# Masking decays by a minimum on VectorE, and moving copies and mask products to ScalarE, in a gated DeltaNet stage

## The chip, the cores and the metric

The program runs on one core of a Trainium2 chip. The engines of the core are named here as in the profile: PE is TensorE, DVE is VectorE, ACT is ScalarE, POOL is GpSimd, SP is SyncE, which issues the DMA transfers. The metric is the device time of one execution in microseconds (us), lower being better.

## The reference, cut to what matters

Two different transformer blocks run one after the other on a 1024 x 1024 activation. The first mixes tokens with a bidirectional gated DeltaNet (4 head pairs of 64 channels, chunks of 64 tokens) beside a spatial gating unit, then has a feed-forward part; the second is an S5 state-space block with a gated feed-forward. All products are in float32.

```
for l in range(DEPTH):
    h = rms_norm(x, norm_mix[l])
    proj = jnp.einsum("bsd,dc->bsc", h, w_in[l])
    q, k, v, z, b_f, b_b, a_f, a_b, su, sv = jnp.split(proj, SPLIT_POINTS, axis=-1)
    qkv = jax.nn.silu(short_conv(jnp.concatenate([q, k, v], axis=-1), conv_w[l]))
    o_a = bidir_gated_deltanet(qkv, z, b_f, b_b, a_f, a_b, a_log_fwd[l], dt_bias_fwd[l],
                               a_log_bwd[l], dt_bias_bwd[l], gdn_norm[l])
    o_b = spatial_gating(su, sv, sgu_v_norm[l], sgu_w[l], sgu_b[l], sgu_out_norm[l])
    mix = jnp.concatenate([o_a, o_b], axis=-1)
    x = x + jnp.einsum("bsc,cd->bsd", mix, w_out[l])
```

The change touches only the DeltaNet. Within a chunk of 64 tokens a decay matrix exp(g_i - g_j) weights the products of keys with keys and of queries with keys. It holds only for j on one side of i (lower triangle for the forward direction, upper for the backward one); elsewhere it must be zero.

## The kernel before, in words

Every float32 product is made of three products of split operands (high and low part); ACT writes the high part (line 318) and DVE the low part (line 319), for weights (`wr` to `wh`, `wl`) and activations.

The first stage, up to about 750 us, weaves two kinds of work on PE. One is dense work: the projections `mm` of line 611, whose weights come in pieces of 256 KB. The other is the DeltaNet of four head pairs, `pair_gdn`, of which two are open at a time (named L and R; pairs 0 and 2 use the buffers of L, pairs 1 and 3 those of R). A planner (`drive`) writes PE's instructions in a fixed order that follows estimated latencies; each engine runs its own instructions in order. The order on DVE, ACT and SP is set by the framework's scheduler when the program is built, so that an edit can move neighbouring instructions there.

For each pair the projections of q, k and v are taken out of PSUM on DVE (`raw`, line 753), convolved over tokens (lines 759 on ACT, 763 and 766 on DVE, result `cy` or a slot of `fbgkq`) and normalised; line 824 (ACT) and lines 826 and 830 (DVE) make the rows of log decays, which go to DRAM and come back spread over 64 partitions. Then `pair_gdn` runs these steps:

- decay: for four matrices (two kinds in `N` and `Am`, two directions; the tiles are named `ca`, `fbgkq`, `ca`, `de` in the profile) DVE adds a column term (line 899), POOL overwrites the forbidden triangle with -1e30 by two selects, one for each half of the partitions (line 903), and ACT takes the exponential (line 905).
- token_major: PE transposes keys (and later values) into PSUM (line 881, `tp`), eight pieces of 64 x 256 are copied to SBUF, half of them by ACT (line 887) and half by DVE (line 889).
- gram: PE multiplies keys and queries (`gram`, line 773), DVE multiplies by the decays (line 925).
- inverse: DVE inverts 32 x 32 triangles by 31 dependent steps (lines 955 and 957, tiles `stp` and `h`), transposes the result (lines 962, 963, 965) and masks it by two products with a constant of halves (line 968).
- lvl, wu, chain, out: small products on PE, with copies out of PSUM on ACT (lines 985 to 1044), a recurrence over chunks (lines 1072, 1075) and the output norm (lines 1107 to 1120; line 1111 is ACT's spread of the norm's factor, which PE then transposes as `orb`).

After that stage come the output projection, the feed-forward parts and the second block, which the change does not touch.

Of the kernel before, what the change touches and what calls it, by code (L numbers as in the profile page):

```python
# [7 lines left out]
F32 = mybir.dt.float32  # L8
F32R = mybir.dt.float32r
I32 = mybir.dt.int32  # L10
AF = mybir.ActivationFunctionType
ALU = mybir.AluOpType
# [4 lines left out]
P = 128  # L17
# [5 lines left out]
NC = 16  # L23
NEG = -1.0e30
# [102 lines left out]
class Ln:  # L127
# [77 lines left out]
    def bc(self):  # L205
        K = self.K
        self.rb = K.bcast(self.dgr)
        m = K.bcast(self.dgm)
        self.mb = K.tmp("cb")[:, :m.shape[-1]]
        K.A.activation(self.mb, m, AF.Copy)  # L210
# [41 lines left out]
class Kern:  # L252
# [396 lines left out]
    def gdn_consts(self):  # L649
        gc, I, V, G, A = self.gc, self.I, self.V, self.G, self.A  # L650
        self.rows = gc.tile([P, S], F32, tag="rows", name="rows", bufs=1)
        self.bk = gc.tile([P, 32], F32, name="bk")
        self.dma(self.bk, I["c_bk"])
        self.bq = gc.tile([P, 32], F32, name="bq")
        self.dma(self.bq, I["c_bq"])
        self.half2 = gc.tile([P, 2 + 48], F32, name="half2")[:, :2]
        self.dma(self.half2, I["c_half"])
        self.selc = gc.tile([P, 12], F32, name="selc")
        self.dma(self.selc, I["c_selc"])
        self.cwh = gc.tile([P, 60], F32, name="cwh")  # L660
        o, c = VOFF["conv"]
        V.tensor_scalar(self.cwh, self.vecs[:, o:o + c], 0.5, None, op0=ALU.mult)
        self.mcol = gc.tile([32, 1], F32, name="mcol")
        A.activation(self.mcol, self.vec("g_alog")[:32], AF.Exp)
        V.tensor_scalar(self.mcol, self.mcol, -1.0, None, op0=ALU.mult)
        self.heads = gc.tile([P, 2], F32, name="heads")
        G.memset(self.heads, 0.0)
        for h in range(2):
            G.memset(self.heads[64 * h:64 * h + 64, h:h + 1], 1.0)
        self.gh = gc.tile([P, 1], F32, name="gh")  # L670
        V.tensor_scalar(self.gh, self.vec("gdn_gain"), 0.5, None, op0=ALU.mult)

# [183 lines left out]
    def pair_gdn(self, p, st, R):  # L856
        V, A, G, T = self.V, self.A, self.G, self.T
        (kq, vtd), rd, col = st
        c3 = lambda t: t.rearrange("p (c k) -> p c k", k=64)
# [15 lines left out]
        def token_major(dst, src):  # L875

            d4 = dst.rearrange("p (b e k) -> p b e k", e=2, k=64)
            for h in range(2):
                ps = self.gps(R, [P, 4, 2, 64], "tp")
                for b in range(4):  # L880
                    T.transpose(ps[:, b].rearrange("p h k -> p (h k)"), src[:, (4 * h + b) * P:(4 * h + b + 1) * P], self.ident)
                yield 0.55, 0.0
                for e in range(2):
                    for hh in range(2):
                        o, i = d4[64 * hh:64 * hh + 64, 4 * h:4 * h + 4, e, :], ps[64 * e:64 * e + 64, :, hh, :]
                        if e == hh:
                            A.activation(o, i, AF.Copy)
                        else:
                            V.tensor_copy(o, i)

        N, Am = [a, b], [c_, d_]
        for v in range(2):
# [3 lines left out]
        for v in range(2):  # L896
            for d in range(2):
                rb = (N, Am)[v][d]
                self.late(V.tensor_tensor(c3(rb), c3(rb), bc(d), op=ALU.add))
                for hh in range(2):  # L900
                    sl = slice(64 * hh, 64 * hh + 64)
                    sg = 1 if d == 0 else -1
                    G.affine_select(c3(rb)[sl], c3(rb)[sl], pattern=[[0, NC], [sg, 64]], compare_op=ALU.is_ge,
                                    fill=NEG, base=0, channel_multiplier=-sg)
                A.activation(rb, rb, AF.Exp)
        yield 0.0, 5.0
        while p >= 2 and p - 2 not in self.done:
            yield 0.0, 3.0
        kp = e_
        yield from token_major(kp, K)  # L910
        yield 0.0, self.LAT_TM

# [48 lines left out]
        yc = K.rearrange("p (d c k) -> p d c k", d=2, k=32)  # L961
# [3 lines left out]
        V.transpose(f, K)  # L965
        Y = [g, hs]
        for d in range(2):
            V.tensor_tensor(Y[d].rearrange("p (c e k) -> p c e k", e=2, k=32),
                              yc[:, d].unsqueeze(2).to_broadcast([P, NC, 2, 32]),
                              self.half2.unsqueeze(1).unsqueeze(3).to_broadcast([P, NC, 2, 32]), op=ALU.mult)  # L970
        yield 0.0, 4.0

        self.mark(f"lvl{p}")
# [50 lines left out]
        W, U = [f, K], Y  # L1024
        KW = [a, kp]
        yield from token_major(vp, vt)
        yield 0.0, self.LAT_TM
        for d in range(2):
# [36 lines left out]
        for st in range(1, NC + 1):  # L1065
            if st < NC - 1:
                cp = [self.gps(R, [P, 64], "cp", d) for d in range(2)]
                for d in range(2):
                    c = (st, NC - 1 - st)[d]
# [7 lines left out]
            if st >= 9:  # L1077

                k = st - 9
                if k % 4 == 0:  # L1080
                    while self.held:
                        yield 0.0, 0.5
                    o = self.gps(R, [P, 8, 64], "ob", 2)
# [29 lines left out]
        for h in range(2):  # L1113
            rb = self.gps(R, [P, 4, P], "orb")
# [3 lines left out]
            sl = self.HS[h]  # L1118
# [1206 lines left out]
```

## Time and profile before

| | |
|---|---|
| median of 3 runs | 2756.83 us (2752.54 to 2758.98) |
| the profiled execution's own time | 2753.74 us |
| its span in the trace | 2751.8 us |
| busy shares of the span | PE 95%, DVE 67%, ACT 38%, POOL 10% |
| mean granted clock of PE, share of full speed | 0.969 |

The busy shares are means over the span. The page also cuts the span into 40 slices of 69 us; the first ten hold most of the stage that the change touches, and PE's digit there (its busy share in tenths) is between 6 and 9, where it is 9 in almost all later slices.

### The profile page before, as it was taken

The page shows a single profiled execution, that of the slowest core. Times are in us where ns is not written, and L with a number is a line of the kernel's source. Part 1 is how long each engine was busy: PE and PEld are TensorE (multiplying, and loading weights), DVE is VectorE, ACT ScalarE, POOL GpSimd, SP SyncE. Part 2 cuts the span into 40 slices and gives each one's busy share as a digit, 9 for nine tenths or more (in the row PEclk, how much of TensorE's full clock was granted, in tenths as well). Part 3 has the DMA queues.
Part 4 walks back from the last instruction along what each step waited for, and adds up shares of the span by engine and source line. Part 5 has one row for each costly group of instructions (what it writes and reads, how often), then busy time and mean ns, then how long its engine had stood idle before and what let it go on. Part 6 is the DMA issues. An engine that isn't in the chain of part 4 may idle for free.

```text
span 2751.8 us, 39513 instructions
## 1 busy us (share of the span) xinstructions
PE 2602.0 (95%) x14952; PEld 2088.2 (76%) x14952; DVE 1854.9 (67%) x3367; ACT 1044.6 (38%) x1721; POOL 279.5 (10%) x502
## 2 busy tenths in 40 slices
PE   7868988898899999999999999989999999999997
PEld 5656766676688888888788888868876888888885
DVE  7899768865696566655548778666597555564456
ACT  5433443432454445221236433452253333351222
POOL 0220011000000000299700001100000000000010
PEclk9989999999999999999999999999999999999998
DMA  3332143131234336454413624644322222242211
GB/s 104 101 93 66 56 119 108 46 126 40 86 105 139 117 105 209 125 169 151 140 53 115 197 95 150 200 163 136 113 67 73 88 74 91 92 166 80 92 47 61
DMA packets 298621, 299.71 MB, mean 109 GB/s; under 512 B 34912, under 2 KB 243936, under 8 KB 298176
## 3 DMA queue, kind: packets, MB, share of 16 engines
q1 hardware_dynamic: 298432, 297.20, 34.3%
q8 instruction: 117, 1.92, 0.3%
q14 instruction: 72, 0.59, 0.1%
HBM read 222.29 MB, written 74.58 MB: 108 GB/s over the span
## 4 chain that ended last, share of the span: by engine, by line
PE 75%; DVE 14%; DMA 3%; ACT 3%; issue 3%; POOL 1%; SPq 1%; ACTq 0%; DVEq 0%; POOLq 0%
PE mm L1325 34%; PE mm L1298 26%; PE mm L611 6%; PE wu L773 2%; DVE wl L319 1%; DVE stp L955 1%; DVE h L957 1%; DVE cy L763 1%; PE ob L773 1%; PE cp L773 1%; DVE res L216 1%; PE mm L1430 0%; DVE res L215 0%; PE mm L193 0%; DVE t L319 0%
## 5 line engine op out<-in xcount | busy, mean ns | idle before, releaser
L1325 PE MATMUL mm<-t,wh 128*128 128x512 f32 x1728 | 541.4, 394 | 11.9 <-DVE acc L1372 4.5
L318 ACT ACTIVATE wh<-wr 128x512 fp32r<-128x512 f32 (+1 forms) x386 | 236.1, 614 | 660.9 <-PE mm L1298 280.8
L319 DVE TENSOR_TENSOR wl<-wr,wh 128x512 fp32r<-128x512 f32 (+1 forms) x385 | 267.4, 695 | 214.1 <-ACT wh L318 212.9
L1325 PEld LDWEIGHTS mm<-t,wh 128*128 128x128 f32 x1728 | 325.6, 189 | 88.6 <-DVE acc L1372 6.5
L1325 PE MATMUL mm<-b,wh 128*128 128x512 f32 x1232 | 382.4, 392 | 3.3 <-ACT acc L1366 3.2
L1298 PE MATMUL mm<-fh,wh 128*128 128x512 f32 x880 | 345.2, 392 | 3.7 <-DVE res L1506 3.7
L1298 PE MATMUL mm<-fl,wh 128*128 128x512 f32 x880 | 342.5, 389 | 0.0
L1298 PE MATMUL mm<-fh,wl 128*128 128x512 f32 x880 | 342.5, 389 | 0.0
L1325 PE MATMUL mm<-t,wl 128*128 128x512 f32 x864 | 338.2, 391 | 0.0
L1325 PEld LDWEIGHTS mm<-b,wh 128*128 128x128 f32 x1232 | 231.6, 188 | 53.7 <-ACT acc L1366 4.6
L1325 PE MATMUL mm<-b,wl 128*128 128x512 f32 x616 | 240.2, 390 | 0.0
L318 ACT ACTIVATE wh<-ws 128x512 fp32r<-128x512 f32 x216 | 135.4, 630 | 256.6 <-PE mm L1325 233.4
L1298 PEld LDWEIGHTS mm<-fh,wh 128*128 128x128 f32 x880 | 165.2, 188 | 40.8 <-issue 4.0
L319 DVE TENSOR_TENSOR wl<-ws,wh 128x512 fp32r<-128x512 f32 x216 | 148.5, 690 | 70.2 <-ACT wh L318 69.9
L1298 PEld LDWEIGHTS mm<-fh,wl 128*128 128x128 f32 x880 | 165.2, 188 | 34.7
L1298 PEld LDWEIGHTS mm<-fl,wh 128*128 128x128 f32 x880 | 165.2, 188 | 34.1 <-issue 0.5
L1325 PEld LDWEIGHTS mm<-t,wl 128*128 128x128 f32 x864 | 163.4, 189 | 33.9
L611 PE MATMUL mm<-xh,wh 128*128 128x512 f32 (+1 forms) x400 | 172.0, 430 | 12.8 <-ACT wh L318 7.2
L611 PE MATMUL mm<-xl,wh 128*128 128x512 f32 (+1 forms) x400 | 168.0, 420 | 2.1 <-DVE xl L399 2.0
L611 PE MATMUL mm<-xh,wl 128*128 128x512 f32 (+1 forms) x400 | 168.8, 422 | 0.0
L1506 DVE TENSOR_TENSOR res<-mm,res 128x512 f32<-128x512 f32 x128 | 85.8, 683 | 74.1 <-PE mm L1298 74.1
L1325 PEld LDWEIGHTS mm<-b,wl 128*128 128x128 f32 x616 | 115.9, 188 | 24.5
(491 smaller groups left out, 4273.1 us busy)
## 6 DMA issues: line engine op xcount, KB each, us to landing
wr<-in_w_ff SPq DMA_DIRECT2D x76, 256.0 KB
wr<-in_w_ff SPq DMA_DIRECT2D x32, 512.0 KB
fl<-ffd SPq DMA_DIRECT2D x32, 512.0 KB
wr<-in_w_in SPq DMA_DIRECT2D x32, 512.0 KB
wr<-in_w_in SPq DMA_DIRECT2D x60, 256.0 KB
wr<-in_w_gate SPq DMA_DIRECT2D x22, 512.0 KB
wr<-in_w_up SPq DMA_DIRECT2D x22, 512.0 KB
fl<-hd SPq DMA_DIRECT2D x22, 512.0 KB
```

Source lines behind the costliest of these rows:

```text
L216: K.V.tensor_tensor(r, r, self.mb, op=ALU.subtract)
L318: self.A.activation(hi, src, AF.Copy)
L319: return (lo_eng or self.V).tensor_tensor(lo, src, hi.bitcast(F32), op=ALU.subtract)
L611: self.T.matmul(ps, a[:, t, :], b[:, sl], start=(first and j == 0), stop=(last and j == 2))
L763: V.scalar_tensor_tensor(y[:, a:b], raw[:, a + o:b + o], cw[:, k:k + 1], y[:, a:b], op0=ALU.mult, op1=ALU.add)
L773: self.T.matmul(out(s), lhsT(s), rhs(s), start=start, stop=stop)
L955: V.tensor_tensor(tm, X3[:, :, 0:j, j:j + 1].to_broadcast([P, 2, j, n]), T3[:, :, j:j + 1, m:16].to_broadcast([P, 2, j, n]), op=ALU.mult)
L957: V.tensor_tensor(T3[:, :, 0:j, m:16], T3[:, :, 0:j, m:16], tm, op=ALU.subtract)
L1298: self.T.matmul(ps, a, b[:, sl], start=(start and k + j == 0), stop=(stop and k == n - 1 and j == 2))
L1325: self.T.matmul(ps, a[:, k, :], b, start=(start and k + j == 0), stop=(k == 3 and j == 2), skip_group_check=True)
L1506: V.tensor_tensor(res[d][:, sl], self.mm(w, ffs[g], sl), res[d][:, sl], op=ALU.add)
```

## The change

Four edits, all in the DeltaNet. A constant `below` (128 x 2 x 64) is made once at the start: +1e30 where a decay is allowed, -1e30 where it isn't, one plane for each direction. The decays are masked by one minimum with that constant on DVE in place of two selects on POOL. All eight copies of each token_major group go to ACT, where four were on DVE. The two mask products behind the inverse become four scaled copies on ACT, one for each direction and half.

```
+        self.below = gc.tile([P, 2, 64], F32, name="below")
+        G.memset(self.below, -NEG)
+        for d in range(2):
+            for hh in range(2):
+                sl = slice(64 * hh, 64 * hh + 64)
+                sg = 1 - 2 * d
+                G.affine_select(self.below[sl, d, :], self.below[sl, d, :], pattern=[[sg, 64]], compare_op=ALU.is_ge,
+                                fill=NEG, base=0, channel_multiplier=-sg)
...
-                        if e == hh:
-                            A.activation(o, i, AF.Copy)
-                        else:
-                            V.tensor_copy(o, i)
+                        A.activation(o, i, AF.Copy)
...
-                for hh in range(2):
-                    sl = slice(64 * hh, 64 * hh + 64)
-                    sg = 1 if d == 0 else -1
-                    G.affine_select(c3(rb)[sl], c3(rb)[sl], pattern=[[0, NC], [sg, 64]], compare_op=ALU.is_ge,
-                                    fill=NEG, base=0, channel_multiplier=-sg)
+                V.tensor_tensor(c3(rb), c3(rb), self.below[:, d:d + 1, :].to_broadcast([P, NC, 64]), op=ALU.min)
                 A.activation(rb, rb, AF.Exp)
...
-            V.tensor_tensor(Y[d].rearrange("p (c e k) -> p c e k", e=2, k=32),
-                              yc[:, d].unsqueeze(2).to_broadcast([P, NC, 2, 32]),
-                              self.half2.unsqueeze(1).unsqueeze(3).to_broadcast([P, NC, 2, 32]), op=ALU.mult)
+            for e in range(2):
+                A.activation(Y[d].rearrange("p (c e k) -> p c e k", e=2, k=32)[:, :, e, :], yc[:, d], AF.Copy,
+                             scale=self.half2[:, e:e + 1])
```

PE's order of instructions is the same before and after, row for row. DVE, ACT and SP are reordered by the scheduler. In the rows of the changed kernel below, lines stand lower by 9 up to the decays and by 2 behind them: its 905, 906 and 907 are the add, the minimum and the exponential, 772 is line 763 of before, 927 is 925, 957 and 959 are 955 and 957.

The first place is DVE at the decays of pair 1, in the middle of the inverse of pair 0. Before:

```order
L899 TENSOR_TENSOR ca<-ca,col 128x1024
L899 TENSOR_TENSOR fbgkq<-fbgkq,col 128x1024
L899 TENSOR_TENSOR ca<-ca,col 128x1024
L899 TENSOR_TENSOR de<-de,col 128x1024
L955 TENSOR_TENSOR stp<-fbgkq,h 128x240
L766 SCALAR_TENSOR_TENSOR cy<-raw,cy 128x1024
L319 TENSOR_TENSOR wl<-wr,wh 128x512
L949 TENSOR_TENSOR i<-i,fbgkq 128x1024
L753 TENSOR_TENSOR z<-mm,rb 128x512
L925 TENSOR_TENSOR ca<-gram,ca 128x256 x2
L957 TENSOR_TENSOR h<-h,stp 128x2x20x6
L925 TENSOR_TENSOR fbgkq<-gram,fbgkq 128x256 x2
```

After, from the same first add on:

```order
L905 TENSOR_TENSOR ca<-ca,col 128x1024
L772 SCALAR_TENSOR_TENSOR cy<-raw,cwh,cy 128x1023
L957 TENSOR_TENSOR stp<-fbgkq,h 128x240
L906 TENSOR_TENSOR ca<-ca,below 128x1024
L905 TENSOR_TENSOR fbgkq<-fbgkq,col 128x1024
L772 SCALAR_TENSOR_TENSOR cy<-raw,cwh,cy 128x1023
L959 TENSOR_TENSOR h<-h,stp 128x2x20x6
L906 TENSOR_TENSOR fbgkq<-fbgkq,below 128x1024
L905 TENSOR_TENSOR ca<-ca,col 128x1024
L772 SCALAR_TENSOR_TENSOR cy<-raw,cwh,cy 128x1022
L927 TENSOR_TENSOR ca<-gram,ca 128x256
L957 TENSOR_TENSOR stp<-fbgkq,h 128x266
```

The four adds stood together; now each add and its minimum are apart by a convolution step or an inverse step, and the fourth add and its minimum come 4 and 11 rows below the last row shown.

The second place is ACT at the decays of pair 0, where line 824 (833 after) takes pair 1's key norms out of PSUM. Before:

```order
L905 ACTIVATE ca<-ca 128x1024
L905 ACTIVATE fbgkq<-fbgkq 128x1024
L905 ACTIVATE ca<-ca 128x1024
L318 ACTIVATE wh<-wr 128x512
L824 ACTIVATE rows<-l_886 32x512 x2
L905 ACTIVATE de<-de 128x1024
L765 ACTIVATE raw<-fbgkq 128x1024
L887 ACTIVATE de<-tp 64x4x64 x2
L805 ACTIVATE raw<-fbgkq 128x1024
L887 ACTIVATE de<-tp 64x4x64 x2
```

After:

```order
L907 ACTIVATE ca<-ca 128x1024
L318 ACTIVATE wh<-wr 128x512
L907 ACTIVATE fbgkq<-fbgkq 128x1024
L318 ACTIVATE wh<-wr 128x512
L833 ACTIVATE rows<-l_880 32x512 x2
L907 ACTIVATE ca<-ca 128x1024
L895 ACTIVATE de<-tp 64x4x64 x8
L774 ACTIVATE raw<-fbgkq 128x1024
L907 ACTIVATE de<-de 128x1024
```

The norms' copy stood behind three exponentials and stands now behind two; the eight transposed keys' copies go as one group ahead of the last exponential.

The third place is ACT at the decays of pair 3, where line 1111 (1113 after) spreads the output norm's factor of pair 1. Before:

```order
L905 ACT_TABLE_LOAD
L905 ACTIVATE ca<-ca 128x1024
L1224 ACTIVATE vss<-st 128x4
L318 ACTIVATE wh<-wr 128x512
L1111 ACTIVATE h<-qy 128x1024
L1166 ACT_TABLE_LOAD
L1166 ACTIVATE sv<-sv 128x1024
L905 ACT_TABLE_LOAD
L905 ACTIVATE fbgkq<-fbgkq 128x1024
L905 ACTIVATE ca<-ca 128x1024
L887 ACTIVATE de<-tp 64x4x64 x4
```

After:

```order
L907 ACT_TABLE_LOAD
L907 ACTIVATE ca<-ca 128x1024
L1226 ACTIVATE vss<-st 128x4 x2
L318 ACTIVATE wh<-wr 128x512
L907 ACTIVATE fbgkq<-fbgkq 128x1024
L1168 ACT_TABLE_LOAD
L1168 ACTIVATE sv<-sv 128x1024
L907 ACT_TABLE_LOAD
L907 ACTIVATE ca<-ca 128x1024
L1113 ACTIVATE h<-qy 128x1024
L895 ACTIVATE de<-tp 64x4x64 x8
```

The spread stood ahead of two table loads, the Gelu of line 1166 and two exponentials, and stands now behind them.

## Rows read from the trace of the kernel before

**Rows 1.** Part 1 of the page: busy us, share of span, instructions.

```profile
PE 2602.0 (95%) x14952; PEld 2088.2 (76%) x14952; DVE 1854.9 (67%) x3367; ACT 1044.6 (38%) x1721; POOL 279.5 (10%) x502
```

**Rows 2.** Windows: length, busy us of PE, PEld, DVE, ACT, POOL, then clock, DMA.

```profile
100.00:125.00 25.00, 19.97 (x83) 14.69 (x82) 22.07 (x23) 11.99 (x16) 15.54 (x8) 0.93 0.55 144
125.00:150.00 25.00, 24.24 (x141) 18.12 (x142) 21.79 (x33) 10.97 (x15) 0.00 (x0) 0.93 0.16 43
...
175.00:200.00 25.00, 11.04 (x74) 8.34 (x72) 24.86 (x30) 9.75 (x13) 13.86 (x8) 0.77 0.09 31
...
225.00:250.00 25.00, 20.12 (x181) 16.70 (x183) 24.80 (x63) 3.53 (x5) 0.00 (x0) 0.87 0.22 74
...
275.00:300.00 25.00, 24.77 (x351) 18.87 (x351) 20.52 (x35) 11.22 (x23) 0.00 (x0) 1.00 0.09 33
```

**Rows 3.** PE's waits, 0 to 750 us: for whom, total us, times, longest.

```profile
PE gram L773 <- DVE de L925: 15.0, 1, 15.0
...
PE wu L773 <- ACT fbgkq L1037: 4.6, 1, 4.6
...
PE mm L611 <- ACT rows L824: 3.6, 1, 3.6
...
PE wu L773 <- ACT fbgkq L1033: 2.7, 1, 2.7
...
PE mix L1211 <- DVE vq L1203: 2.6, 1, 2.6
...
PE gram L773 <- ACT de L887: 2.2, 1, 2.2
```

**Rows 4.** Timeline of DVE, 100 to 215 us: start, duration, instruction.

```profile
107.94 2.15 DVE L763 SCALAR_TENSOR_TENSOR fbgkq<-raw,cwh,fbgkq 128x1022 f32<-128x1022 f32 x1
...
119.84 1.62 DVE L319 TENSOR_TENSOR wl<-wr,wh 128x512 fp32r<-128x512 f32 x1
...
183.64 1.22 DVE L899 TENSOR_TENSOR fbgkq<-fbgkq,col 128x1024 f32<-128x1024 f32 x1
184.78 2.15 DVE L899 TENSOR_TENSOR ca<-ca,col 128x1024 f32<-128x1024 f32 x1
...
197.24 1.18 DVE L957 TENSOR_TENSOR h<-h,stp 128x240 f32<-128x240 f32 x1
...
201.91 0.44 DVE L955 TENSOR_TENSOR stp<-fbgkq,h 128x272 f32<-128x272 f32 x1
202.39 0.44 DVE L957 TENSOR_TENSOR h<-h,stp 128x272 f32<-128x272 f32 x1
```

**Rows 5.** Timeline of POOL, 95 to 500 us, pair 1's first selects.

```profile
183.84 4.09 POOL L903 TENSOR_SCALAR_AFFINE_SELECT ca<-ca 64x1024 f32<-64x1024 f32 x2 [62.92 <-DVE ca L899]
```

**Rows 6.** Timeline of ACT, 100 to 275 us; in brackets idle before, and releaser.

```profile
116.81 1.06 ACT L905 ACTIVATE ca<-ca 128x1024 f32<-128x1024 f32 x1 [2.34 <-POOL ca L903]
...
118.41 1.18 ACT L824 ACTIVATE rows<-l 32x512 f32<-32x512 f32 x2
...
122.98 0.65 ACT L887 ACTIVATE de<-tp 64x256 f32<-64x256 f32 x2
...
137.45 1.27 ACT L936 ACTIVATE ca<-ca 32x512 f32<-32x512 f32 x2 [7.50 <-DVE ca L925]
```

**Rows 7.** Instructions of lines 889 and 968: durations in ns, lowest, median, highest.

```profile
L889 DVE COPY de<-tp x16: 417/422/427, 124.2 to 472.9; 64x256 f32<-64x256 f32 x16
...
L968 DVE TENSOR_TENSOR fbgkq<-fbgkq,half x4: 1212/1217/1224, 246.0 to 545.0; 128x1024 f32<-128x1024 f32 x4
```

**Rows 8.** Timeline of ACT, 352 to 400 us, at pair 2's decays.

```profile
365.68 1.06 ACT L905 ACTIVATE fbgkq<-fbgkq 128x1024 f32<-128x1024 f32 x1 [1.21 <-POOL fbgkq L903]
...
366.91 0.38 ACT L1037 ACTIVATE fbgkq<-wu 128x256 f32<-128x256 f32 x1
```

**Rows 9.** Timeline of ACT, 440 to 560 us, at pair 3's decays.

```profile
464.49 1.06 ACT L1111 ACTIVATE h<-qy 128x1024 f32<-128x1024 f32 x1 [1.41 <-DVE qy L313]
465.56 1.28 ACT L1166 ACT_TABLE_LOAD   x1
```

## The prediction

> **What bounds the kernel now.** I read the shares first [rows 1]: PE is busy 95% of the span, DVE 67%, ACT 38%, POOL 10%. By these means DVE and POOL have time to spare. The second view is a table of windows [rows 2], and it tells another story for the stage that the change touches. From 175 to 200 us PE works 11.04 of 25 us while DVE works 24.86; from 225 to 250 us DVE is again at 24.80 and PE at 20.12. From 275 to 300 us PE is at 24.77 and DVE no longer full. So the first stage alternates between stretches that DVE bounds and stretches that PE bounds, and what DVE saves counts only in the first kind. The granted clock is 0.77 and 0.87 in the two DVE windows, that is, partly at 1.2 GHz after PE had stood, and 1.00, all at 2.4 GHz, where PE never stood.
>
> The third view is PE's waits [rows 3]. The longest is one of 15.0 us for the product of line 925, of pair 1: PE needs a bank that only DVE's fourth decay product gives free, and the fourth decay is the last thing in DVE's crowded queue. The others that the change comes near are of 2 to 5 us, and four of these name ACT. The timeline of ACT says why in two places: at 116.81 us the exponential of line 905 begins only after 2.34 us of waiting for POOL, and the copy of line 824, on which PE waits 3.6 us, stands behind it [rows 6]; at 365.68 us the same happens, and line 1037, on which PE waits 4.6 us, comes next but one [rows 8].
>
> **The change part by part.** *Decays.* Removed from POOL: 32 selects; two of them take 4.09 us [rows 5]. Added to DVE: 16 minima of 128 x 1024 with a constant that is repeated along the middle dimension. No row shows a minimum. The nearest is the add of line 899, of the same size and also with a repeated operand, 1.22 us [rows 4], started 1.14 us apart (183.64 and 184.78). That repeating along the middle is free is seen at lines 955 and 957: 0.44 us for 272 columns with it and without it. The bounds are therefore 1.14 us from below and, were the minimum to run as slowly as an add beside POOL, 2.15 us from above; I take 1.14, as no POOL select is left to slow it. That is 4.6 us for each pair.
>
> Against it stands what the selects cost DVE itself. Beside them the same add takes 2.15 in place of 1.22 us [rows 4]. In pair 1 seven DVE instructions, the first at 184.78 us and the last at 197.24 us (1.18 us for a 240-column step whose larger like takes 0.44), are together 6.3 us longer than their kind elsewhere; in pair 0 it is seven between 107.94 and 119.84 us, 4.5 us in all. I count nothing of the kind in pairs 2 and 3, where DVE has gaps.
>
> *Copies.* 32 copies leave DVE at 0.42 us [rows 7], 1.7 us for each group of four. On ACT two of them take 0.65 us [rows 6], so ACT gets 1.3 us more in each of eight groups, but its four no longer wait for DVE's four.
>
> *Mask products.* Two of 1.22 us [rows 7] leave DVE for each pair, 2.3 us in steps of 1.14, and one of the two stood ahead of the transpose on which PE's next product waits. ACT gets four copies of 128 x 512 scaled by a column. The nearest rows are two copies of 32 x 512 in 1.27 us, 0.64 each [rows 6]. For 128 partitions the bounds are 0.59 us (a copy of 32 x 512 from PSUM, 1.18 for two [rows 6]) and 1.06 (the exponential of twice the columns); I take 0.64, or 2.5 us a pair. They run beside the transpose of line 965 and the product behind it, and delay the next copy out of PSUM if they take over 3 us.
>
> Now the sum, by place.
>
> Pair 0, 100 to 150 us. ACT's line 824 moves ahead of the third exponential, so the wait of 3.6 us can go whole; the wait of 2.2 us for the copied keys goes in part; and the clock of 0.93 in both windows [rows 2], at 1.2 GHz for a while after the first of these waits, costs 0.07 x 50 = 3.5 us, which goes with it. That is 9.3 us at most. DVE bounds it too: it has 6.1 us idle in the 50 us, and its own load falls by 4.5 + 1.7 - 4.6 = 1.6 us, 7.7 in all. I take **6**; the lower bound is 0, if the weights' loads hold PE in place.
>
> Pair 1 and the end of pair 0's inverse, 168 to 265 us, with DVE full. DVE's load changes by -6.3 (slowed instructions) + 4.6 (minima) - 1.7 (pair 1's keys) - 1.7 (pair 0's values) - 2.3 (pair 0's masks) = -7.4 us. As PE waits for DVE within and at the end of this stretch (the 15.0 us), I take **7**. The lower bound is 3: by the new order the first 925 product of `de` gains only 1 to 3 us, since convolution steps that stood ahead of the adds are now among them, and the rest could be lost behind it.
>
> Pair 2, 357 to 368 us. Line 1037 needs two exponentials to pass; the second is free after two adds and two minima on DVE, 4 x 1.14 us after the start of the first add, and no longer after POOL. That leaves about half of the 4.6 us: **2.5**, bounds 0 and 4.6.
>
> Pair 3, 456 to 480 us. Here the order hurts: line 1111 ran at 464.49 us, just ahead of a table load of 1.28 us [rows 9], and now stands behind an exponential, the load, the Gelu, a second load and another exponential, 1.06 + 1.28 + 1.06 + 1.28 + 1.06 = 5.7 us by the rows for such instructions [rows 6, 9]. Its input also comes about 1 us later on DVE, behind minima. On the other side the last decay is ready sooner, without POOL. I take **-2**, bounds -5.7 and 0.
>
> Pair 2's values and products, 500 to 517 us. Four copies of DVE, 1.7 us, stand ahead of line 1203, on which PE waits 2.6 us, and line 1033, on which it waits 2.7 us, moves ahead of a table load and two exponentials. Of these 5.3 us I take **2.5**.
>
> Sum: 6 + 7 + 2.5 - 2 + 2.5 = 16 us. From the profiled execution's 2753.74 us this makes 2737.7; the median of the runs stands 3.1 us above that execution, so the forecast for the median is **2741 us**. PE's order is unchanged and PE bounds the rest, so time won in the first stage stays won.
>
> One rule of the Trainium skill speaks against the change. What the windows show is above: DVE full and PE at 44% from 175 to 200 us [rows 2]. The page Perfetto Trace Analysis, section Identifying the Most-Contended Engine, has the engine with the highest occupancy as the one to optimise first. Here that is PE with 95%, and relieving DVE would bring nothing, 2757 us in place of 2741. The same page's section Optimization Strategy allows for regimes with different engines, and the rows of this trace are of that kind.
>
> **The rivals.** *Hidden anyway: 2757 us.* The mean shares are right, and what DVE gives back is taken up by the next wait: weight loads in pair 0, a spread of decays through DRAM in pair 1. For it speak PE's 95%; against it the 15.0 us, which end on DVE's product with DVE busy all through. This is also the case of the page's rule just named. Chance 0.12.
>
> *Only DVE's own saving: 2749 us.* The gains in ACT's order (6 in pair 0, 2.5 in pair 2) fail, since they rest on ACT passing its copies a few microseconds sooner; 16 - 8.5 = 7.5 us are left. Chance 0.13.
>
> *ACT's added work comes out as PE waits: slower.* ACT gets 8 x 1.3 + 4 x 2.5 = 20.4 us, all in order ahead of copies out of PSUM that PE waits for. If all of it lands on PE, and PE's clock falls from 1.00 to 0.87 as in the window from 225 us [rows 2] over, say, 150 us of this stage, this costs 20.4 + 0.13 x 150 = 40 us, and the kernel takes 2756.8 - 16 + 40 = 2781 us. It is slower than before by 0.2% from the point where over 21.5 of these 40 us arrive. Against it: ACT works less than half of every window shown, and it waited for DVE's copies within these groups before. Chance 0.09.
>
> That the change doesn't do what it says is excluded by the order: POOL's 32 selects are gone, and four small ones at the start remain.
>
> **How the numbers follow.** The forecast case (a gain of 9 us or more) has 0.66. Its own range adds the terms' ends: gains of 3 in the second place and 6 in all others together, 9 us, or 27 us: 2730 to 2748. The measurement of this kernel can tell about 0.2%, or 5.5 us, from no change. Faster by more than that: 0.66 and two thirds of the second rival, 0.75. Within it: the first rival and the rest of the second, 0.16. Slower: 0.09. The range of 2725 to 2757 us reaches below the largest sum by what a steadier clock may add, and up to no change, leaving out the slower case and about half of the first rival.
>
> **What would show it.** In the changed profile DVE's adds take 1.22 us everywhere and the minima the same; PE's 15 us wait for line 925 falls below 13 us; the wait for line 824 is gone and the clock from 100 to 150 us is above 0.95; PE's wait for line 1111's `orb` grows. The prediction is wrong if a minimum takes 2 us, if ACT's scaled copies take 1 us, or if new waits of PE for ACT of 5 us or more appear between 275 and 350 us.

## The result, and the profile after

The changed kernel takes 2721.96 us (median; 2719.84 to 2723.69) where the kernel before, beside it on the same chip, takes 2754.68 us (2750.56 to 2758.98). The ratio is 0.9881, with a 95% interval of 0.9862 to 0.9900: 33 us faster, twice the 16 us of the forecast's sum, and 3 us below the range. The profiled execution took 2720.45 us with a span of 2718.4 us.

The page's shares, against [rows 1]: DVE lost 21 us of work and POOL 51, ACT gained 21.5, and PE, which does the same work, is busy 8 us less because more of it ran at 2.4 GHz.

```profile
PE 2593.9 (95%) x14952; PEld 2082.0 (77%) x14952; DVE 1833.9 (67%) x3343; ACT 1066.1 (39%) x1769; POOL 228.1 (8%) x475
```

The windows that answer to [rows 2], with the same columns:

```profile
100.00:125.00 25.00, 24.97 (x146) 18.97 (x145) 24.10 (x31) 16.95 (x25) 0.00 (x0) 1.00 0.52 143
125.00:150.00 25.00, 23.76 (x110) 18.27 (x109) 24.60 (x42) 11.82 (x15) 0.00 (x0) 0.88 0.37 95
...
175.00:200.00 25.00, 14.85 (x100) 10.24 (x99) 24.62 (x47) 9.46 (x12) 0.00 (x0) 0.80 0.16 50
...
225.00:250.00 25.00, 22.53 (x355) 18.05 (x355) 23.17 (x55) 11.58 (x21) 0.00 (x0) 0.93 0.26 82
...
275.00:300.00 25.00, 24.91 (x506) 17.86 (x504) 16.95 (x43) 11.85 (x21) 0.00 (x0) 1.00 0.19 59
```

From 100 to 125 us PE now never stands (24.97 in place of 19.97 us) and keeps 2.4 GHz. From 175 to 200 us DVE is as full as before, yet PE gets 14.85 us of work done and not 11.04.

PE's waits, 0 to 750 us, answering to [rows 3]:

```profile
PE gram L782 <- DVE de L927: 10.7, 2, 10.2
PE l L826 <- ACT raw L814: 7.2, 1, 7.2
PE orb L1118 <- ACT h L1113: 7.1, 2, 6.7
...
PE rb L1234 <- DVE sv L1228: 6.2, 2, 3.7
...
PE mm L611 <- DVE rows L835: 5.1, 1, 5.1
...
PE cp L782 <- DVE ca L1077: 2.5, 4, 1.2
```

Further rows of the same view of the kernel before, on which readings below rest:

```profile
PE rb L1232 <- DVE sv L1226: 6.7, 3, 5.2
...
PE l L817 <- ACT raw L805: 5.5, 1, 5.5
...
PE cp L773 <- DVE ca L1075: 4.2, 4, 1.9
...
PE wu L773 <- ACT fbgkq L887: 3.1, 1, 3.1
...
PE orb L1116 <- ACT h L1111: 2.7, 2, 2.3
...
PE cp L773 <- DVE de L1075: 2.4, 2, 1.5
...
PE mm L611 <- DVE rows L826: 1.1, 1, 1.1
```

The 15.0 us have become 10.2. The waits for lines 824, 887, 1033 and 1203 are gone, and 1037's (4.6 us, now 1039) is 1.1. Longer are the waits for the norm's factor (`orb`, 6.7 for 2.3), for pair 2's norms (`l`, 7.2 for 5.5) and for DVE's `rows` (5.1 for 1.1).

The timelines of ACT and of DVE at pair 0's decays show the new order at work: the eight copies run in one piece of 3.12 us, and a minimum takes what an add takes, 1.22 us, started 1.13 us after the instruction ahead.

```profile
113.27 1.19 ACT L833 ACTIVATE rows<-l 32x512 f32<-32x512 f32 x2
115.58 1.06 ACT L907 ACTIVATE ca<-ca 128x1024 f32<-128x1024 f32 x1 [1.12 <-DVE ca L906]
116.65 3.12 ACT L895 ACTIVATE de<-tp 64x256 f32<-64x256 f32 x8
...
105.87 1.22 DVE L906 TENSOR_TENSOR ca<-ca,below 128x1024 f32<-128x1024 f32 x1
107.00 1.22 DVE L905 TENSOR_TENSOR fbgkq<-fbgkq,col 128x1024 f32<-128x1024 f32 x1
```

**Where the time came from.** PE's instructions stand in the same order in all these kernels, so the start of the same matmul in two traces can be subtracted. The timeline of PE shows how, first in the kernel before, then in the changed one:

```profile
500.05 1.11 PE L881 MATMUL tp<-ident,ca 128*128 128x128 f32 x4 [4.08 <-ACT h L999]
507.13 2.05 PE L1211 MATMUL mix<-ws,vq 128*128 128x128 f32 x16 [2.65 <-DVE vq L1203]
516.33 1.92 PE L773 MATMUL wu<-fbgkq 64*64 64x128 f32 x16 [2.72 <-ACT fbgkq L1033]
```

```profile
476.31 1.12 PE L890 MATMUL tp<-ident,ca 128*128 128x128 f32 x4 [4.08 <-ACT h L1001]
482.07 2.05 PE L1213 MATMUL mix<-ws,vq 128*128 128x128 f32 x16
488.46 1.09 PE L782 MATMUL wu<-fbgkq 64*64 64x128 f32 x16
```

The lead is 23.7 us at the first row, 25.1 at the second and 27.9 at the third, and both waits are gone. Done for all matmuls, in us gained against before (places by the time of before, one execution of each kernel; the totals also hold the small stretches left out, none over 2.2 us):

| place, us | forecast | change | minimum alone | copies alone | masks alone | minimum + copies | copies + masks |
|---|---|---|---|---|---|---|---|
| 100 to 150 | 6 | 9.0 | 3.2 | 2.7 | -1.0 | 8.3 | 2.7 |
| 150 to 171 | - | -3.5 | -0.4 | -0.3 | 0.2 | -2.8 | 0.4 |
| 171 to 265 | 7 | 9.8 | -2.4 | 4.2 | 2.2 | 8.7 | 4.6 |
| 265 to 300 | - | 1.4 | -1.6 | -6.0 | -0.1 | -3.2 | -4.3 |
| 300 to 321 | - | 1.7 | 0.0 | 1.7 | 0.0 | 1.8 | 1.8 |
| 357 to 368 | 2.5 | 2.5 | 2.5 | 0.7 | 0.6 | 2.3 | 0.7 |
| 415 to 437 | - | 3.2 | 0.0 | 0.0 | 3.2 | 1.6 | 1.5 |
| 456 to 480 | -2 | -0.8 | -0.8 | 0.5 | -1.3 | -1.9 | 0.4 |
| 500 to 524 | 2.5 | 7.3 | -1.5 | 7.3 | -1.1 | 1.1 | 7.3 |
| 524 to 700 | - | -0.3 | 5.0 | 2.3 | 0.7 | 7.5 | 2.4 |
| 100 to 700 | 16 | 30.7 | 3.5 | 10.8 | 3.6 | 23.5 | 17.1 |

The table ends at 700 us because behind it single executions of these kernels differ by -3 to +4 us, though nothing was changed there. PE's idle time between 100 and 700 us fell by 22 us (76 to 55, from the gaps between its matmuls); the other 9 us of the 30.7 are matmuls that ran at 2.4 and no longer at 1.2 GHz (granted clock 0.937 over this stretch, 0.923 before).

### The profile page after: what moved, and what is told of

Same layout as the page of the kernel before. It is cut to its first block, busy times and chain, and to the rows that moved or that the text cites. A ratio compares the mean times of both kernels' runs of the same rounds, so it can differ in the third digit from the quotient of the medians.

```text
span 2718.4 us, 39435 instructions
## 1 busy us (share of the span) xinstructions
PE 2593.9 (95%) x14952; PEld 2082.0 (77%) x14952; DVE 1833.9 (67%) x3343; ACT 1066.1 (39%) x1769; POOL 228.1 (8%) x475
## 4 chain that ended last, share of the span: by engine, by line
PE 72%; DVE 12%; DMA 4%; POOL 4%; issue 3%; ACT 3%; SPq 2%; ACTq 0%; POOLq 0%; DVEq 0%
PE mm L1327 34%; PE mm L1300 22%; PE mm L611 9%; PE wu L782 2%; DVE wl L319 1%; PE ob L782 1%; PE cp L782 1%; DVE res L215 1%; DVE stp L957 1%; DVE h L959 1%; DVE res L216 1%; SPq L1709 1%; PE mm L1432 0%; DVE cy L772 0%; DMA wr<-in_w_out 0%
```

## The experiments

| kernel | median us | ratio to before, 95% interval |
|---|---|---|
| the change | 2721.96 | 0.9881 (0.9862 to 0.9900) |
| minimum alone | 2746.32 | 0.9965 (0.9951 to 0.9980) |
| copies alone | 2739.12 | 0.9934 (0.9919 to 0.9949) |
| masks alone | 2748.39 | 0.9965 (0.9952 to 0.9978) |
| copies + masks | 2736.98 | 0.9931 (0.9916 to 0.9946) |
| minimum + copies | 2731.18 | 0.9908 (0.9893 to 0.9923) |
| change, minima twice | 2732.84 | 0.9919 (0.9905 to 0.9934) |
| change, ACT's copies twice | 2746.86 | 0.9969 (0.9957 to 0.9980) |
| change, DVE copies too, for nobody | 2717.65 | 0.9867 (0.9850 to 0.9883) |
| change, copies by halves | 2733.65 | 0.9920 (0.9905 to 0.9935) |
| change, POOL busy beside pair 0 | 2723.86 | 0.9883 (0.9867 to 0.9900) |
| change, spread on POOL | 2726.08 | 0.9890 (0.9873 to 0.9906) |
| the same, exponentials 4 steps later | 2722.51 | 0.9883 (0.9866 to 0.9899) |
| the same, 12 steps later | 2724.07 | 0.9882 (0.9864 to 0.9900) |
| minimum + copies, exponentials 4 steps later | 2737.96 | 0.9937 (0.9922 to 0.9952) |

**The parts.** Three kernels make one edit of the diff each and leave the others out.

> The kernel before with the decays' minimum alone; copies and mask products stay on DVE. Theory A (the gain is POOL's: its selects held up the exponentials and slowed DVE beside them): 18 to 26 us of the 32.7 us come back, most of it by 135 us (9 us) and from 168 to 210 us (5 to 7 us). Theory B (the gain is DVE's load, 4.0 us a pair given to ACT, while the minima put 4.6 us a pair on DVE): no more than 10 us. Theory C (neither alone, each lifts one of two limits of the same stretches): under 12 us here and the three parts alone sum to under 22 us.

> The kernel before with all eight copies of each transposed group on ACT, and POOL's selects kept. Theory A: 4 to 8 us, mainly at 168 to 200 us and from 500 to 517 us. Theory B: 12 to 18 us. The rival of the prediction that ACT's added work comes out as PE's waits: slower by 5 us or more.

> The kernel before with the two mask products behind each inverse on ACT alone. Theory A: 2 to 5 us, as one of the two products stood ahead of a transpose on which PE waits (3.1 us at 260 us). Theory B: 4 to 9 us. If PE waits elsewhere then: within 2 us of before.

Measured: about 10, 18 and 10 us (ratio times 2757). Theory A, that POOL was the cause, falls: its own edit brings a third. By times B looks right, and C falls as it was put, since the three sum to 37 us, give or take 7 (their intervals combined in quadrature). In the three profiled executions alone they sum to 26.6 us (8.9, 13.5 and 4.2) where the change's has 33.3, so whether the times add up is not settled. The places do not: at 100 to 150 us the parts have 3.2, 2.7 and -1.0, and the change has 9.0. How one edit can leave the copies late is seen in the minimum alone, in the timelines of ACT and DVE at pair 0's values (within the place of 171 to 265 us):

```profile
260.87 0.38 ACT L896 ACTIVATE fbgkq<-tp 64x256 f32<-64x256 f32 x1 [6.64 <-DVE fbgkq L898]
261.27 1.15 ACT L768 ACTIVATE cy<-raw,cwh 128x1024 f32<-128x1024 f32 x1
263.19 0.38 ACT L896 ACTIVATE fbgkq<-tp 64x256 f32<-64x256 f32 x1 [0.76 <-DVE fbgkq L898]
...
259.98 0.86 DVE L898 COPY fbgkq<-tp 64x256 f32<-64x256 f32 x2
```

ACT and DVE copy in turn, and here a copy of ACT waited 6.64 us until DVE, busy with inverse steps and a product, had made its two. The group of eight copies took 10.4 us from start to end, for 3.2 us of work. In the kernel before, the eight groups took 2.6 to 7.7 us. What ACT waited for ahead of line 887 in that kernel sums it up, 15.3 us for DVE:

```profile
its engine sat idle before it (us, times) until:
  DVE fbgkq L889: 10.8, 6
  PE tp L881: 4.8, 5
  DVE de L889: 4.5, 6
```

Two pairs of edits follow:

> Copies and mask products on ACT, decays masked by POOL's selects as before: the changed kernel without its minimum. If the parts add up: 27 us faster than before (17.9 + 8.7), so 5 to 6 us behind the changed kernel. If the minimum is needed for the shorter wait of 15 us (in each single part that wait stayed at 14.2 to 15.4 us, with all three it is 10.2): the wait stays above 14 us and the gain is 20 us or less.

> Minimum on DVE and all copies on ACT; the mask products stay on DVE (the changed kernel without its fourth edit). Interlock theory (the decays of a pair and its copies meet in one product, so each alone leaves the other late): the lead of pair 0 at 135 us is 8 to 9 us, where each alone had 3, the 15 us wait is 10 to 11 us, and the kernel is 24 to 31 us faster than before. If the parts only add up: 6 us at 135 us, a wait above 14 us, and 24 us at most in all.

Without the minimum the change keeps 19 us, and the wait for line 925 stays at 15.1 us; with minimum and copies, 25 us are there, that wait is 10.1 us and pair 0 has 8.3 us. So the first two places need both: the product waits for a decay (add, mask, exponential) and for the copied keys, and each edit alone left the other late (only the wait for line 824 goes with the minimum alone). By times the masks, about 10 us alone, add 1 us to the copies and 7 to minimum and copies; such differences carry an uncertainty of 6 to 7 us. The masks' own place is 415 to 437 us, where the recurrence (`cp`) waits 4.2 us for DVE in the kernel before, 2.6 with the masks alone and 2.5 in the change, and still 4.2 with minimum and copies.

**The price of DVE's and of ACT's time.**

```
# minima twice: the added line stands once more
+                V.tensor_tensor(c3(rb), c3(rb), self.below[:, d:d + 1, :].to_broadcast([P, NC, 64]), op=ALU.min)
# ACT's copies twice
                         A.activation(o, i, AF.Copy)
+                        A.activation(o, i, AF.Copy)
# DVE copies too
+                        if e != hh:
+                            V.tensor_copy(self.dum[64 * hh:64 * hh + 64].rearrange("p (b k) -> p b k", k=64), o)
# copies by halves
-                        A.activation(o, i, AF.Copy)
+                        if h == 0:
+                            A.activation(o, i, AF.Copy)
+                        else:
+                            V.tensor_copy(o, i)
```

> The changed kernel with every minimum made twice (16 more of 1.14 us on DVE, 18.2 us, 4.6 us a pair; the value is the same). Load theory (in this stage PE waits for DVE's time, wherever it is saved): 8 to 14 us slower than the changed kernel, about half of the added time. Rival (the order of the instructions on ACT and DVE matters, not DVE's load): within 4 us.

> The changed kernel with each of the eight copies of a transposed group made twice on ACT (64 more, some 0.39 us each, 25 us more of ACT; the value is the same). Load theory (DVE binds, ACT has room): 0 to 6 us slower than the changed kernel, as only the copies ahead of PE's next product are late by 3.1 us. Rival (ACT's work comes out as PE's waits): 20 us slower or more.

> The changed kernel, all copies on ACT, but DVE makes four copies of each group as well, into a scratch tile that nobody reads (32 copies of 64 x 256, 13 us or less). It tells the two reasons for the copies' 18 us apart. Load theory (DVE's time was given back): 7 to 14 us slower than the changed kernel. Latency theory (PE's product no longer waits for the four copies in DVE's queue): within 4 us of the changed kernel.

> The changed kernel, but of each transposed group the first four copies are ACT's and the last four DVE's, so that ACT and DVE hand over once and not four times; ACT has the load of before, DVE too. Theory queue (what costs is that copies stand in DVE's queue behind minima): 10 to 20 us slower than the changed kernel. Theory hand-over (what costs is ACT and DVE waiting for each other in turn): within 5 us of the changed kernel.

18.2 us more of minima cost 11 us. 24 us more of ACT's copies (64 of 0.378 us) cost 25 us: the rival mechanism of the prediction is real at nearly its full price, in other amounts. PE's waits of that kernel show it at the places where a group or the copy behind it is waited for:

```profile
PE wu L782 <- ACT fbgkq L1036: 8.3, 2, 4.9
...
PE gram L782 <- ACT de L896: 7.8, 2, 5.4
```

But the copies that DVE makes for nobody, 9 us (32 of 0.288) of the 13.5 us (32 of 0.42) that the change took off it, cost nothing: 4 us less than the change, with intervals that overlap. So DVE's load as such was not, in the main, what the copies relieved. What is left is the waiting: ACT's 15.3 us for DVE's copies, and PE's 2.2 and 3.1 us for line 887, all of which are gone. Half of each group back on DVE costs 12 us, which fits the theory of the queue by its time, but not by its places. Up to 500 us this kernel is 3.2 us behind the change (20.5 us of gain for 23.7), with 1.6 us of it at pair 0 and nothing at 171 to 265 us, though its groups take 5.2 and 5.4 us at pairs 0 and 1, where DVE is full, and 2.0 to 3.5 us elsewhere. Most of the rest is the place of 500 to 524 us, where it loses 1.7 us and the change gains 7.3, for another reason (below); 3.6 us of that are back by 700 us. So the queue and the hand-overs are not told apart: one hand-over in place of four cost 3 us or so up to 500 us.

**POOL's selects beside DVE.** A scratch tile is selected over by POOL while DVE makes pair 0's decays; all other engines keep the order of the changed kernel.

```
+        if p == 0:
+            G.tensor_copy(self.dum[:, 0:1], col[:, 0, 2:3])
+            for k in range(32):
...
+                G.affine_select(c3(self.dum)[sl], c3(self.dum)[sl], pattern=[[0, 4], [1, 64]], compare_op=ALU.is_ge,
+                                fill=NEG, base=0, channel_multiplier=-1)
```

> The changed kernel, and beside pair 0's decays POOL works for some 16 us on a scratch tile that nobody reads (32 selects of 64 x 256); the order on PE, ACT and DVE is that of the changed kernel row for row. Theory A1 (POOL's work slows DVE, and DVE's time in this stretch is PE's): adds and minima of pair 0 take about 2 us in place of 1.22, the lead over before at 135 us falls from 9.0 to 4 or 5 us, and the kernel takes 4 to 5 us more than the changed one. Theory A2 (only the wait of the exponentials for POOL's result mattered): DVE is slowed as much, but the lead at 135 us stays at 8 to 9 us and the time within 1 us of the changed kernel.

> As the run with POOL's work beside pair 0's decays, with 16 selects of 64 x 512 in place of 32 of 64 x 256. If POOL slows DVE in proportion to how much of the time it moves data: adds and minima take 1.5 to 1.9 us where they took 1.42. If the size of a select does not matter: 1.42 again.

The timelines of DVE, selects of 256 columns first, then of 512:

```profile
107.41 1.42 DVE L913 TENSOR_TENSOR fbgkq<-fbgkq,col 128x1024 f32<-128x1024 f32 x1
...
118.14 0.68 DVE L764 TENSOR_TENSOR raw<-mm,rb 128x512 f32<-128x512 f32 x1
```

```profile
107.64 1.67 DVE L913 TENSOR_TENSOR fbgkq<-fbgkq,col 128x1024 f32<-128x1024 f32 x1
```

The add takes 1.22 us alone, 1.42 and 1.67 beside these, and 2.15 beside selects of 1024 columns [rows 4]; both theories had expected about 2 us beside the smallest. Pair 0's gain falls from 9.0 to 7.5 us with the small selects and to 3.8 us with the larger ones, so DVE's slowing does reach PE there. Yet the first kernel's time stays within 2 us of the changed one, inside the uncertainty, and the second's one execution took 2722.43 us: at 700 us the lead is only 3 us smaller (27.8 and 27.6 for 30.7), and what is lost at pair 0 is partly won back later (at 524 to 700 us both gain 2.4 us, where the change loses 0.3).

**The order on ACT.** The change's largest surplus is 500 to 524 us, whole in some kernels and absent in others. Two edits move ACT's instructions there: the norm's spread goes to POOL, and the exponentials of line 950 are issued later.

```
-        A.activation(c3(sq), r.unsqueeze(2).to_broadcast([P, NC, 64]), AF.Copy)
+        G.tensor_copy(c3(sq), r.unsqueeze(2).to_broadcast([P, NC, 64]))
...
-        for eg, dst in ((i_, i_), (K, Q)):
-            self.late(A.activation(eg, eg, AF.Exp))
-            V.tensor_tensor(dst, eg, Q, op=ALU.mult)
...
+            if j == 25:
+                for eg, dst in ((i_, i_), (K, Q)):
+                    self.late(A.activation(eg, eg, AF.Exp))
+                    V.tensor_tensor(dst, eg, Q, op=ALU.mult)
```

> The changed kernel with the spread of the norm's factor (1113, on which PE waits 6.7 us for pair 2) on POOL, which is idle there, so that it no longer stands behind ACT's table load and exponentials. If that queue is the cause: the wait falls to 2 us or less and the kernel is 3 to 4 us faster than the changed one, 2718 us. If the spread's own input is late: no change. If POOL needs over 5 us for it: slower.

> The changed kernel with the spread on POOL, and the exponentials behind the decays' sums (950, with their table load) issued four of the inverse's steps later, so that ACT's copy 1035 stands ahead of the load and not behind it. Theory order (the 500 to 524 us place is worth 6 to 7 us when 1035 passes the table load and the two exponentials, and nothing otherwise): the gain there is 6 to 8 us, where the spread alone on POOL had 0.8, and the kernel takes 2716 to 2720 us. Rival (that place follows DVE's work, not ACT's order): 0 to 2 us there, 2725 us.

> As the run before, with these exponentials twelve of the inverse's steps later, behind all copies of that product. Theory order: 6 to 8 us at 500 to 524 us again; the later products with the exponentials may cost DVE some of it elsewhere: 2714 to 2724 us. Rival: 0 to 2 us there.

> Minimum and copies without the fourth edit (mask products on DVE), and the exponentials of 950 four steps later, so that ACT's copy 1035 passes the table load. Theory order: the place of 500 to 524 us gains 6 to 7 us where the same kernel had 1.1 us with the old order, and the kernel takes 2724 to 2727 us. Rival (the fourth edit itself brings that place): 1 to 2 us there, 2731 us.

With the spread on POOL alone (1.04 to 2.09 us a piece) the wait for it falls only from 6.7 to 4.5 us, so most of it is the spread's own late input. And 500 to 524 us gains 0.8 us where the change has 7.3. ACT's timeline there, first of that kernel, then of the one with the exponentials four steps later:

```profile
490.24 1.28 ACT L950 ACT_TABLE_LOAD   x1
491.54 1.06 ACT L950 ACTIVATE i<-i 128x1024 f32<-128x1024 f32 x1
492.50 1.04 ACT L950 ACTIVATE fbgkq<-fbgkq 128x1024 f32<-128x1024 f32 x1
493.56 1.08 ACT L1035 ACTIVATE fbgkq<-wu 128x512 f32<-128x512 f32 x2
```

```profile
488.30 0.59 ACT L1036 ACTIVATE fbgkq<-wu 128x512 f32<-128x512 f32 x1
490.49 0.60 ACT L1036 ACTIVATE fbgkq<-wu 128x512 f32<-128x512 f32 x1 [1.59 <-PE wu L782]
491.10 1.28 ACT L959 ACT_TABLE_LOAD   x1
492.39 1.06 ACT L959 ACTIVATE i<-i 128x1024 f32<-128x1024 f32 x1
```

In the three kernels in which the first copies of 1035 stand ahead of the load this place gains 7.5, 7.5 and 7.1 us; with the old order it had 0.8 and 1.1. The other traces agree. Of all sixteen kernels, nine have a copy of this product ahead of the load, as the change has, and gain 6.5 to 7.5 us at the place; the seven others gain -1.7 to 1.1. That settles the place, but not what it is worth in the end. From 524 to 700 us the nine gain between -0.3 and 5.3 us and the seven between 0.7 and 7.5. Minimum and copies, without the early copy, gain 7.5 us there: PE's waits for the spatial gating's `sv` (its product `rb`), 6.5 us before and 6.2 in the change in this stretch, are gone in that kernel. From 500 to 700 us in all it has 8.6 us, more than the change with 7.0, and with the move 8.4. For the kernels with the spread on POOL the move is worth 3.5 us by 700 us (9.9 for 6.4), and 3.6 us by the medians. The last kernel is slower than without the move, since the later exponentials cost time elsewhere: it loses 7.7 us at 265 to 300 us, and without the move 3.2. None of these versions is faster than the changed kernel by more than the intervals.

Why a wait of 3 us makes a difference of 6 to 7 us at this place is seen on PE, in the timeline and windows of the kernel with minimum and copies alone:

```profile
496.00 0.40 PE L611 MATMUL mm<-xh,wh 128*128 128x512 f32 x1
496.23 0.40 PE L611 MATMUL mm<-xl,wh 128*128 128x512 f32 x1
500.04 1.09 PE L782 MATMUL wu<-fbgkq 64*64 64x128 f32 x16 [3.41 <-ACT fbgkq L1035]
...
503.54 0.63 PE L611 MATMUL mm<-xl,wh 128*128 128x512 f32 x1
503.96 0.63 PE L611 MATMUL mm<-xh,wl 128*128 128x512 f32 x1
```

```profile
490.00:500.00 10.00, 6.47 (x58) 5.23 (x58) 8.34 (x21) 5.68 (x8) 0.00 (x0) 1.00 0.17 41
500.00:512.00 12.00, 11.96 (x68) 9.83 (x70) 8.92 (x29) 1.56 (x5) 0.00 (x0) 0.57 0.00 1
```

Ahead of the wait the matmuls start 0.23 us apart; behind it 0.42, at a granted clock of 0.57, that is nearly all at 1.2 GHz. In the changed kernel, which does not wait there, they stand 0.23 us apart behind the same product.

## Why the prediction was wrong in size

The direction and most mechanisms were right; the sum was half of what came. Two steps of the sum failed. Its term for pair 2's values took half of two waits and nothing for the clock (2.5 us, where 7.3 came), and it had no terms at all for PE's shorter waits (7.0 us came).

*Pair 0: "I take 6" of at most 9.3.* It gained 9.0: close to the ceiling of PE's waits, and over the 7.7 us that the prediction allowed for DVE, which is idle for 1.3 us of these two windows now and not 6.1. The wait for line 824 and the one for the copied keys are gone. The reason given, ACT's order and 1.6 us of DVE's load, was incomplete, since minimum and copies had to come together. But 3.5 us were given back at once, at 150 to 171 us: half of it because PE now waits 7.2 us for pair 2's norms (5.5 before), half because matmuls ahead of that run 0.43 us apart, at 1.2 GHz, and not 0.23. This is the next limit: of the nine kernels that gain over 7 us at pair 0, eight lose 0.4 to 3.9 us behind it, and the one with doubled minima, which loses 4.3 us at pair 0, gains 6.2 us here.

*Pair 1: 7.* 9.8 us came, or 6.3 with the loss just ahead of it. DVE stayed full, as forecast, and the 15.0 us fell below 13. But the 4.8 us won at that wait were lost again at 212 to 216 us of before, where the lead falls by 6 us: PE now waits 5.1 us for DVE's `rows`, 1.1 before, and runs at 1.2 GHz behind it. The gain that lasted came behind this, at waits that the prediction did not price: line 887's 3.1 us for pair 0's values, 2.7 of the 4.9 us ahead of `zp`, behind the inverse, and 2.4 us for DVE's `z`, with the clock behind these waits. So the 7 came near by the load it counted, not by the wait it named. "Hidden anyway", the first rival, was right for these two places, 150 to 171 and 212 to 216 us.

*Pair 2: 2.5* came as 2.5, from the minimum alone. *Pair 3: -2* came as -0.8: 3.4 us were lost at the spread, which did go behind the table loads, with its own input late as well, and 2.6 us came back behind it.

*Pair 2's values: "Of these 5.3 us I take 2.5".* This is the single term that was most mis-sized: 7.3 us came. Both waits went whole, 5.3 us, and with them the stretch at 1.2 GHz behind the second, about 3 us, less 1 us of clock ahead of the first. The prediction counted the clock at pair 0 and left it out here. In the change it stayed, with -0.3 us from 524 to 700 us; but kernels without it won up to 7.5 us there, so it is worth less to the whole kernel than it measures at its place.

*Places not listed.* These make up the largest part of the surplus, and the sum put them at nothing without giving a reason. 265 to 321 us brought 3.1 us (1.7 of it from a wait of 1.5 us of the recurrence for DVE, gone with the copies) and 368 to 437 us 3.9 us (3.2 of it the recurrence again, by the masks). Short waits of PE for DVE and ACT were in the same view as the long ones and were not added up.

So the surplus of 14.7 us is about 4.8 at the values, 7.0 at unlisted places, 2.8 at pair 1 and 1.2 at pair 3, less a net 0.5 at pair 0 and some tenths. The second rival, that the gains in ACT's order fail, was the wrong way round. The third priced ACT's time rightly, near one for one; what the prediction set against it held: without the waits for DVE's copies the eight leave ACT in 3.1 us in six of the eight groups, 3.8 and 4.2 in two, for 2.6 to 7.7 us before.

Of the signs named, the adds, the minima, the shorter wait, the lost wait for line 824 and the longer `orb` came true. The clock from 100 to 150 us did not reach 0.95: it is 1.00 and then 0.88. ACT's scaled copies take 0.71 us (forecast 0.64).

The prediction read the Trainium skill's page Perfetto Trace Analysis, section Identifying the Most-Contended Engine, as speaking against the change. The page has the engine with the highest occupancy optimised first, and for TensorE the headroom judged by its arithmetic rate or the busy share of its weight loads (PEld, 76%), not by the busy share of its matmuls. It does not say that relieving other engines brings nothing. Its section Optimization Strategy goes on to the gaps of that engine and to what ends them, and these traces agree with that: PE's idle time fell from 76 to 55 us with its work unchanged.

What stays open: each edit lets the scheduler reorder DVE and ACT everywhere, and for places of 1 to 3 us an edit's own effect can't be told from that. How much of the 7.3 us at pair 2's values the change owes to that place alone, and would not have won behind it, is open too.

## What to carry to other kernels

Look for groups of small instructions that two engines share in turn: their price is not only the sum of their durations but each wait for the other engine (10.4 us for 3.2 us of work in the worst group seen), and one engine doing all of them can be quicker though it works more. What added work costs depends on where it stands: 9 us of copies on DVE that nobody waits for cost nothing, 18 us of minima ahead of the exponentials cost 11, and 24 us on ACT ahead of PE's products cost 25. Count a wait of PE with the stretch at 1.2 GHz behind it, and where a wait's cause is removed, start from the whole wait and then ask what is next, rather than halve each. Follow the lead to the end of the stage: what is won or missed at one place can be taken back or made good at a later wait. Add up PE's short waits too: they made up the largest part of what the sum lacked.

## What was not expected of the hardware

The slowing of DVE by POOL grows with the size of one select, not with POOL's being busy: 0.20, 0.45 and 0.93 us more for an add beside selects of 256, 512 and 1024 columns, about 0.9 ns a column, while DVE's instructions with an input from PSUM keep their 0.68 us. In these stretches the two engines alternate, one select to one instruction of DVE with two inputs from SBUF. The shortest selects of these sizes, which ran beside instructions with an input from PSUM, take 0.41, 0.66 and 1.14 us, so each delay is such a select less 0.2 us. The Trainium skill, page SBUF — State Buffer, section Who interferes with whom, describes an exclusive lock between the two engines, held for a whole instruction, which a DVE instruction with two inputs from SBUF needs while POOL reads there; the alternation agrees with it. No run here shows the lock itself.
